# A hybrid decoder step on Trainium2: where 13 fill steps and one tile's weights lie in the mLSTM recurrence

## The chip, the cores and the metric

The kernel runs on one core of one Trainium2 chip. The metric is the device time of one execution, in microseconds (us). A core has several engines that run side by side, each with its own stream of instructions: TensorE (PE) multiplies matrices into PSUM banks and loads the weights for that (PEld), VectorE (DVE) and ScalarE (ACT) do elementwise work and empty PSUM, GpSimd (POOL) does elementwise work too and issues transfers, SyncE (SP) only issues transfers (DMAs). They wait for one another on semaphores.

## The reference

One inference step of a two-layer decoder: an mLSTM layer, then a forgetting-attention layer over one shared K/V, each followed by a SwiGLU FFN. A prompt of 1024 tokens (with 16 meta tokens ahead of it) and 8 requests of 8 new tokens go through the same weights. The change lies in the mLSTM layer, whose mixer is:

```python
def mlstm_chunk(state, inp):
    C, n, m = state
    ...
    s = jnp.einsum('bhtk,bhsk->bhts', q, k) * jnp.exp(dmat - m_t[..., None])
    num = w_inter[..., None] * jnp.einsum('bhtk,bhkv->bhtv', q, C) + jnp.einsum('bhts,bhsv->bhtv', s, v)
    den = w_inter * jnp.einsum('bhtk,bhk->bht', q, n) + jnp.sum(s, axis=-1)
    h = num / jnp.maximum(jnp.abs(den), jnp.exp(-m_t))[..., None]
    ...
    C_new = w_c[..., None, None] * C + jnp.einsum('bhs,bhsk,bhsv->bhkv', w_g, k, v)
    ...
def mlstm_mixer(xn, C0, n0, m0, lead, w_in, b_ig, b_fg, mh_g, w_out):
    p = xn @ w_in
    ...
    h, state = mlstm_sequence(q, k, v, li, lf, state0, lead)
    h = rmsnorm(h.transpose(0, 2, 1, 3), mh_g)
    out = (h.reshape(B, T, HV).astype(xn.dtype) * jax.nn.sigmoid(og)) @ w_out
    return out, state
```

`D_MODEL` is 1024, with 8 mLSTM heads of key width 64 and value width 128. The output gate `og` is a 1024 x 1024 part of the projection `xn @ w_in`. It doesn't depend on the recurrence, only its use does.

## The kernel before

The 1104 tokens (64 of the samples, 16 meta, 1024 of the prompt) lie in nine chunks: chunk 0 has the samples and the meta tokens, 80 in all, and chunks 1 to 8 have 128 each. For the large products they are taken in three groups of three chunks, t = 0, 1, 2, of 336, 384 and 384 columns. To keep float32 accuracy each operand is split into a high and a low part, and each product is three matmuls (`mm3`, lines 193 to 195, the high part of the weights twice, and the low part).

The mixer first makes values, then queries and keys, which go to memory (`qkD`). Then comes `recurrence`, chunk by chunk. For each chunk `chunk_load` brings queries and keys (`qk`), the rows of decays (`eb`) and the weights of the queries (`wb`); `chunk_decay` and an exp make the decay matrix; `chunk_scores` multiplies keys with queries into `sps`, multiplies that with the decay on DVE (L1351), transposes the keys into `kps` (L1355), and scales keys (`kw`, L1357) and queries (`wb`, L1359); `chunk_state` makes the products `cp` for the next state C, and lets POOL decay it (L1395); `chunk_out` makes the products `nps` (from the chunk, and from the state), which ACT copies over the values `vA` (L1420) before it takes the sums of squares (`jk`). Chunk 0 also has the samples, each with its own state `C0`. For them `first_queries` writes the scaled queries to memory (`qwD`, L1367) and reads them back in another layout (`qq`, L1371), and in `chunk_out` DVE places them (L1433) before PE multiplies them with `C0` (L1438).

These products are small and wait for one another. Between them stands **fill**: the output gate's projection, written as a generator, `gates_out`. It has 8 weight tiles, m = 0 to 7, by 3 token groups, by 8 steps, 192 steps in all. One step is three matmuls. Eight steps make one PSUM tile `mmA`; then ACT takes the sigmoid into a staging tile `stg`, and POOL issues its write to memory (`ogD`, L956). The staging tiles are a ring of three. `mmA` has two PSUM banks. `f(n)`, or `g(n)`, called somewhere in the code, issues n steps there. The weights of tile m + 1 are loaded while tile m is in its second group: SP loads them, ACT makes the high part, DVE the low part (L272).

In the last two chunks another piece of work joins. `gate(t)` takes one head of a finished group of chunks, transposes its three chunks into one bank (`ghps`, L1555, which takes its turn in the same two banks as the fill's `mmA`), multiplies it with the gate that was read back from memory (L1556, into `ogqk` or `ogeb`), and splits the product (L271, L272) into the operands of the next stage. In these chunks `g` is defined anew: it calls `gate` each time it is called, and in chunk 8 two fill steps ahead of that. Just before, at the end of chunk 6, a loop issues fill until only the last tile's last group is left (the 184 of the loop's bound).

Within the recurrence the order on PE, DVE, ACT and POOL is that of the code (a manual schedule). Waits come from the data and from memory that is taken over: a tile that lies where an earlier one lay waits for the last use of that one.

The next stage (`mlp`, its products are `pops`) multiplies the gated heads with `w_out`. Its eight weight pairs, m = 0 to 7, high and low, were prepared earlier and are loaded by SP, in order (L512):

```python
for m in range(KT):
    for z in range(2):
        nc.sync.dma_start(ws[m][z].bitcast(F32), self.woD[m][:, z])
```

Pairs 0 to 3 are the tiles `wo2` on the left side of memory, pairs 4 to 7 lie in the `slots` on the right side. The left ones take the memory where the weights of the recurrence's fill and its staging ring had been: pairs 0 and 1 lie over weights, pair 2 over the staging ring. The stage also brings the residual `hD` into the memory of the values (L499, on POOL).

The change touches `gates_out` (its weights' place), `recurrence` (how many steps stand where), `chunk_scores`, `first_queries`, `chunk_state` and `chunk_out`.

Of the kernel before, what the change touches and what calls it, by code (L numbers as in the profile page):

```python
# [12 lines left out]
ALU = mybir.AluOpType  # L13
# [4 lines left out]
P = 128  # L18
D = 1024
KT = D // P  # L20
# [8 lines left out]
NT = len(TT)  # L29
# [8 lines left out]
HA, DK, DV = 8, 64, 128  # L38
# [841 lines left out]
def phase_a(self, vt):  # L880
    nc, I, O = self.nc, self.I, self.O
    w_in = I["w_in_a"][0]
# [3 lines left out]
    with ExitStack() as c3:  # L886
# [48 lines left out]

        def gates_out():

            get = lambda m, later=None: self.load_w([w_in[:, (16 + m) * P : (17 + m) * P]], later=later)
            ws = [get(0)]
            later = []  # L940
# [211 lines left out]
def recurrence(self, kp, rec, v, qkD, fill, gate):  # L1152


    nc, I, O = self.nc, self.I, self.O
    eD, wD, cap, cap0, wcP, wcS, bm = rec
# [4 lines left out]
    def f(n):  # L1161
        for _ in range(n):
            next(fill, None)
            self.fills += 1
# [3 lines left out]
    with ExitStack() as cr, self.pool("recAp", bufs=2, space=PSUM) as pp:  # L1168
# [28 lines left out]
        with self.pool("rec2") as sets[2], self.pool("rec1", bufs=2) as rp, self.pool("rec3") as sets[0]:  # L1197
# [8 lines left out]
            for i in range(1, NT):  # L1206
                N2 = load(i + 2) if i + 2 < NT else None
                if i + 1 < NT:
                    f(12 if i == 1 else 3)
                    self.chunk_scores(i + 1, N, rp, *args, f)  # L1210
# [21 lines left out]
                if i == 6:  # L1232
                    while self.fills < 3 * KT * KT - KT:
                        f(1)

                    def g(n):
                        if i == NT - 1:
                            f(2)
                        gate(0) or gate(1)
                R, N = N, N2  # L1240
# [98 lines left out]
def chunk_scores(self, i, R, rp, pp, kp, C, v, qkD, eD, wD, tm, f):  # L1339
# [10 lines left out]
    for g in range(2):  # L1350
        nc.vector.tensor_tensor(out=eb[:L, g::2, :L], in0=sps[g][:L, :, :L], in1=eb[:L, g::2, :L], op=ALU.mult)  # L1351
    f(2 if i else 6)
# [6 lines left out]
    nc.vector.tensor_tensor(out=qw[:, :, :L], in0=qk[:, :4, :L], in1=qw[:, :, :L], op=ALU.mult)  # L1359


@_add(Net)
def first_queries(self, R, sp):

    nc = self.nc
    qd = self.dram.tile([P, 4, NS], F32, name="qwD")
    nc.gpsimd.dma_start(qd, R["qw"][:, :, :NS])  # L1367
    q2 = R["q2"]
    for a in range(2):
        for z in range(2):  # L1370
            nc.gpsimd.dma_start(q2[a * 64 : a * 64 + 64, :, z, :], qd[z * 64 : z * 64 + 64])  # L1371
    for qm in R["qms"]:
        nc.gpsimd.memset(qm, 0.0)


@_add(Net)
def chunk_state(self, i, R, pp, kp, C, v, qkD, eD, wD, tm, wcP, f):
# [15 lines left out]
    if i + 1 < NT:  # L1393

        nc.gpsimd.tensor_tensor(out=Cw, in0=Cn, in1=wcP[:, :, i].unsqueeze(2).broadcast_to([P, 4, DV + 1]),  # L1395
                                op=ALU.mult)
# [3 lines left out]
def chunk_out(self, i, R, rp, pp, kp, C, v, qkD, eD, wD, tm, den, ssq, f, sp=None, exp=None, then=None):  # L1400
# [22 lines left out]
    if i == 0:  # L1423
        for g, hs in enumerate(((0, 2), (4, 6), (1, 3), (5, 7))):
            f(4)
# [13 lines left out]
            done(ps, g, hs)  # L1439
    else:  # L1440

        for z in range(2):
            f(2 if z == 0 else 3)
# [1596 lines left out]
```

## Time and profile before

| | us |
|---|---|
| median of 3 runs (lowest, highest) | 2829.18 (2827.18, 2837.07) |
| the profiled execution | 2829.72 |
| its span | 2828.0 |
| PE busy, share of the span | 2761.9 (98%) |
| DVE busy | 1800.4 (64%) |
| ACT busy | 1177.3 (42%) |
| POOL busy | 836.0 (30%) |
| mean granted TensorE clock | 0.994 |

The span is the time between the first and the last instruction of the profiled execution; 1.72 us of its time lie outside. Busy time is summed for each engine and says nothing about what it worked beside. Rows of groups give line, engine, operation and tiles (out<-in), the count, the busy time, the mean of one, and what ended the idle time before them, with its amount in brackets. In the timeline the first number is the time in the span, the second the busy time of the piece. `PEclk` is the TensorE clock that was granted, as a share of full speed. Where several instructions run into each other, as PE's matmuls do, a duration contains overlap with its neighbours, and the distance between starts is the pitch.

### The profile page before, as it was taken

What the parts mean: (1) busy time and instruction counts of PE and PEld (TensorE: products, weight loads), DVE (VectorE), ACT (ScalarE), POOL (GpSimd) and SP (SyncE); (2) the same over time, 40 slices, a digit from 0 to 9 for tenths busy, and PEclk for the clock granted to TensorE, in tenths of its full rate; (3) what the DMA queues carried; (4) which work ended last, traced back from release to release, by engine and by line L of the source; (5) the groups of instructions that cost most, each with busy time, mean ns of one, the idle gap of its engine ahead of it and who ended that gap; (6) DMA issues with size and microseconds to landing.
All of it is one profiled execution on the core that took longest, in us unless ns stands there. A gap on an engine that the chain in (4) does not pass through costs nothing. (4 is left out here: it accounts for less than half of the span.)

```text
span 2828.0 us, 60538 instructions
## 1 busy us (share of the span) xinstructions
PE 2761.9 (98%) x23543; PEld 2650.3 (94%) x23543; DVE 1800.4 (64%) x4025; ACT 1177.3 (42%) x2299; POOL 836.0 (30%) x1313
## 2 busy tenths in 40 slices
PE   8999999999999999999999999999999999999998
PEld 8989889999999999999999888677999999999998
DVE  4632566888887765563455444777388888766556
ACT  5422453432322334443444445777343223323345
POOL 3122233132232332124453202544313223323111
PEclk9999999999999999999999999999999999999999
DMA  6666547245554375545444676442524555527556
GB/s 196 171 196 162 144 125 255 90 143 165 176 167 148 112 243 174 195 145 171 139 172 132 237 279 226 154 143 86 157 83 128 175 176 164 161 90 239 178 191 215
DMA packets 439001, 474.03 MB, mean 168 GB/s; under 512 B 41422, under 2 KB 365258, under 8 KB 437690
## 3 DMA queue, kind: packets, MB, share of 16 engines
q1 hardware_dynamic: 387522, 320.78, 36.8%
q0 software_dynamic: 43808, 143.17, 15.3%
q10 hardware_dynamic: 7384, 6.22, 0.7%
q8 instruction: 185, 3.03, 0.5%
q14 instruction: 102, 0.84, 0.1%
HBM read 322.84 MB, written 147.21 MB: 166 GB/s over the span
## 5 line engine op out<-in xcount | busy, mean ns | idle before, releaser
L1611 PE MATMUL m<-xh,slot 128*128 128x276 f32 x2752 | 541.3, 290 | 1.8 <-ACT fs L1640 1.8
L1611 PEld LDWEIGHTS m<-xh,slot 128*128 128x128 f32 x2752 | 440.4, 188 | 3.6 <-ACT fs L1640 2.2
L1611 PE MATMUL m<-xl,slot 128*128 128x276 f32 x1376 | 397.4, 289 | 0.0
L1611 PEld LDWEIGHTS m<-xl,slot 128*128 128x128 f32 x1376 | 259.1, 188 | 0.0
L193 PE MATMUL tmps<-slot,xh 128*128 128x256 f32 (+2 forms) x864 | 243.1, 281 | 0.0
L195 PE MATMUL tmps<-slot,xl 128*128 128x256 f32 (+2 forms) x864 | 240.6, 278 | 0.0
L194 PE MATMUL tmps<-slot,xh 128*128 128x256 f32 (+2 forms) x864 | 240.5, 278 | 0.0
L272 DVE TENSOR_TENSOR slot<-slot,slot 128x1024 fp32r<-128x1024 f32 x124 | 162.9, 1314 | 60.7 <-ACT slot L271 59.2
L271 ACT CAST slot<-slot 128x1024 fp32r<-128x1024 f32 x124 | 129.6, 1046 | 141.2 <-PE m L1611 111.7
L194 PEld LDWEIGHTS tmps<-slot,xh 128*128 128x128 f32 (+1 forms) x864 | 159.2, 184 | 0.1
L195 PEld LDWEIGHTS tmps<-slot,xl 128*128 128x128 f32 (+1 forms) x864 | 158.6, 184 | 0.0
L193 PEld LDWEIGHTS tmps<-slot,xh 128*128 128x128 f32 (+1 forms) x864 | 158.4, 183 | 0.2
L193 PE MATMUL mmA<-xh,whi 128*128 128x384 f32 (+1 forms) x384 | 135.1, 352 | 0.0
L194 PE MATMUL mmA<-xl,whi 128*128 128x384 f32 (+1 forms) x384 | 127.9, 333 | 0.0
L195 PE MATMUL mmA<-xh,wlo 128*128 128x384 f32 (+1 forms) x384 | 127.7, 333 | 0.0
L272 DVE TENSOR_TENSOR slot<-vA,slot 128x1024 fp32r<-128x1024 f32 (+1 forms) x59 | 82.2, 1396 | 32.6 <-ACT slot L271 31.5
L272 DVE TENSOR_TENSOR slot<-Ht,slot 128x1024 fp32r<-128x1024 f32 (+1 forms) x59 | 81.4, 1382 | 32.3 <-ACT slot L271 31.1
L271 ACT CAST slot<-Ht 128x1024 fp32r<-128x1024 f32 (+1 forms) x59 | 61.0, 1037 | 96.8 <-PE m L1611 92.9
L271 ACT CAST slot<-vA 128x1024 fp32r<-128x1024 f32 (+1 forms) x59 | 60.8, 1035 | 95.5 <-PE m L1611 90.5
L1715 DVE TENSOR_TENSOR ws<-ws 128x128 f32<-128x128 f32 x264 | 93.8, 355 | 8.9
L2862 ACT ACTIVATE s<-s,nb 128x272 f32<-128x272 f32 (+7 forms) x126 | 98.9, 786 | 0.0
L2897 ACT COPY th<-tp 128x768 f32<-128x768 f32 (+1 forms) x80 | 73.6, 920 | 53.7 <-PE tp L2889 30.5
(805 smaller groups left out, 8668.8 us busy)
## 6 DMA issues: line engine op xcount, KB each, us to landing
ws<-in_w_down SPq DMA_DIRECT2D x176, 128.0 KB, 2.8
sD<-ws SPq DMA_DIRECT2D x176, 128.0 KB, 2.3
slot<-sD SPq DMA_DIRECT2D x40, 512.0 KB, 4.2
slot<-in_w_gate_up SPq DMA_DIRECT2D x36, 512.0 KB, 3.9
kp<-in_cache_k SPq DMA_DIRECT2D x32, 512.0 KB, 6.7
vp<-in_cache_v SPq DMA_DIRECT2D x32, 512.0 KB, 5.1
vA<-in_w_gate_up SPq DMA_DIRECT2D x26, 512.0 KB, 4.4
Ht<-in_w_gate_up SPq DMA_DIRECT2D x26, 512.0 KB, 3.9
```

What stands on the lines that cost most here:

```text
L193: mm(ps, sh, mh, start=first, stop=False)
L194: mm(ps, sh, ml, start=False, stop=False)
L195: mm(ps, sl, mh, start=False, stop=last)
L271: self.nc.scalar.copy(hi, src)
L272: self.nc.vector.tensor_tensor(out=lo, in0=src, in1=hi.bitcast(F32), op=ALU.subtract)
L1611: nc.tensor.matmul(u.ps[h, b], w[p][:, k], x[q][:, k], start=first and k == i == 0, stop=k == 3 and i == 2, skip_group_check=True)
L1715: tt(out=o, in0=a, in1=b, op=ALU.subtract)
L2862: nc.scalar.activation(ss[z, u], ss[z, u], AF.Exp, bias=nb[:, z : z + 1], accum_out=sm[:, u, z : z + 1])
L2897: nc.scalar.copy(th.rearrange("p x z (u h q) -> p h (x z u) q", h=2, q=64)[:, :, :n], pt[:, :, :n])
```

## The change

- **Weights of m = 7.** A new pool, `gl`, on the right side of memory, takes the high and the low tile of m = 7. They lie where two of the later `slots` are, the low parts of weight pairs 6 and 7 of the next stage.
- **Fill.** Chunk 1 issues 10 steps instead of 12 ahead of chunk 2's scores, chunks 2, 4 and 5 issue 2 instead of 3 there. In `chunk_out` the first half has 1 step instead of 2 in chunks 1, 2, 4 and 5, and in chunk 0 the first of each group's calls has 3 instead of 4. The loop that issued fill at the end of chunk 6 is gone. In the last two chunks, `g` issues one step (chunk 7) or two (chunk 8) before each gate. By the end of chunk 6, 186 steps had been issued before, and 173 now.
- **First queries.** In chunk 0 the queries are scaled ahead of the six fill steps instead of behind the keys; in `first_queries` the two memsets stand ahead of the four reads, which now go by half (z) first; and the first decay of the state on POOL moves from `chunk_state` to `chunk_out`, behind the second of four groups.

```diff
+        gl = c3.enter_context(self.pool("gl", side="right"))
...
-            get = lambda m, later=None: self.load_w([w_in[:, (16 + m) * P : (17 + m) * P]], later=later)
+            get = lambda m, later=None: self.load_w([w_in[:, (16 + m) * P : (17 + m) * P]], later=later,
+                                                    keep=gl if m == 7 else None)
...
-                    f(12 if i == 1 else 3)
+                    f(10 if i == 1 else 2 if i in (2, 4, 5) else 3)
...
                 if i == 6:
-                    while self.fills < 3 * KT * KT - KT:
-                        f(1)
 
                     def g(n):
-                        if i == NT - 1:
-                            f(2)
+                        f(2 if i == NT - 1 else 1)
                         gate(0) or gate(1)
...
+    scale = lambda: nc.vector.tensor_tensor(out=qw[:, :, :L], in0=qk[:, :4, :L], in1=qw[:, :, :L], op=ALU.mult)
+    if i == 0:
+        scale()
     f(2 if i else 6)
...
-    nc.vector.tensor_tensor(out=qw[:, :, :L], in0=qk[:, :4, :L], in1=qw[:, :, :L], op=ALU.mult)
+    if i:
+        scale()
...
-    for a in range(2):
-        for z in range(2):
-            nc.gpsimd.dma_start(q2[a * 64 : a * 64 + 64, :, z, :], qd[z * 64 : z * 64 + 64])
     for qm in R["qms"]:
         nc.gpsimd.memset(qm, 0.0)
+    for z in range(2):
+        for a in range(2):
+            nc.gpsimd.dma_start(q2[a * 64 : a * 64 + 64, :, z, :], qd[z * 64 : z * 64 + 64])
...
-        nc.gpsimd.tensor_tensor(out=Cw, in0=Cn, in1=wcP[:, :, i].unsqueeze(2).broadcast_to([P, 4, DV + 1]),
-                                op=ALU.mult)
+        decay = lambda: nc.gpsimd.tensor_tensor(out=Cw, in0=Cn, in1=wcP[:, :, i].unsqueeze(2).broadcast_to(
+            [P, 4, DV + 1]), op=ALU.mult)
+        if i:
+            decay()
+        else:
+            R["decay"] = decay
...
-            f(4)
+            f(3)
...
             done(ps, g, hs)
+            if g == 1:
+                R["decay"]()
...
-            f(2 if z == 0 else 3)
+            f(3 if z else 1 if i in (1, 2, 4, 5) else 2)
```

The order that results, at three places. First POOL in chunk 0, around the write of the first queries; `qk`, `eb` and `wb` in the last rows are the loads for chunk 1. Before:

```order
L956 DMA ogD<-stg_3194 128x384
L1367 DMA qwD<-wb_3080 512x1x64
L1371 DMA qq<-qwD 64x4x64 x4
L1373 MEMSET qq 128x400 x2
L1395 TENSOR_TENSOR C_107<-C_105,wcP 128x516
L1279 DMA qk_3246<-qkD 128x8x128
L1278 DMA eb_3086<-eD 128x8x128
L1283 DMA wb_3247<-wD 64x4x128 x2
```

And now:

```order
L959 DMA ogD<-stg_3198 128x384
L1371 DMA qwD<-wb_3083 512x1x64
L1374 MEMSET qq 128x400 x2
L1377 DMA qq<-qwD 64x4x64 x4
L1279 DMA qk_3248<-qkD 128x8x128
L1278 DMA eb_3089<-eD 128x8x128
L1283 DMA wb_3249<-wD 64x4x128 x2
L959 DMA ogD<-stg_3264 128x384
L1398 TENSOR_TENSOR C_107<-C_105,wcP 128x516
```

The write of the queries keeps its place behind a write of the gate, the memsets stand ahead of the reads, and the decay of the state (`C_107`) has moved behind the loads of chunk 1 and one more write of the gate.

Second, PE in chunk 7 and 8, from the fifth gate's transposes to chunk 8's state products (`mmA_260` and `mmA_267` are the last tile's groups t = 1 and t = 2 of the changed kernel; the last group of the kernel before is `mmA_262`). Before:

```order
L1555 MATMUL ghps_267_4818<-ident_60,vA_96 128x80
L1555 MATMUL ghps_267_4818<-ident_60,vA_96 128x128 x2
L193 MATMUL mmA_262_4666<-xh_91,whi_253_4353 128x384
L194 MATMUL mmA_262_4666<-xl_92,whi_253_4353 128x384
L195 MATMUL mmA_262_4666<-xh_91,wlo_254_4354 128x384
L1555 MATMUL ghps_269_4852<-ident_60,vA_96 128x80
L1555 MATMUL ghps_269_4852<-ident_60,vA_96 128x128 x2
L1388 MATMUL cp80_4859<-vA_96,kw8_4547 64x129 x4
L1388 MATMUL cp81_4865<-vA_96,kw8_4547 64x129 x4
```

And now:

```order
L1564 MATMUL ghps_265_4793<-ident_60,vA_96 128x80
L1564 MATMUL ghps_265_4793<-ident_60,vA_96 128x128 x2
L193 MATMUL mmA_260_4692<-xh_91,whi_253_4449 128x384
L194 MATMUL mmA_260_4692<-xl_92,whi_253_4449 128x384
L195 MATMUL mmA_260_4692<-xh_91,wlo_254_4450 128x384
L193 MATMUL mmA_267_4827<-xh_91,whi_253_4449 128x384
L194 MATMUL mmA_267_4827<-xl_92,whi_253_4449 128x384
L195 MATMUL mmA_267_4827<-xh_91,wlo_254_4450 128x384
L1564 MATMUL ghps_268_4831<-ident_60,vA_96 128x80
L1564 MATMUL ghps_268_4831<-ident_60,vA_96 128x128 x2
L1392 MATMUL cp80_4838<-vA_96,kw8_4502 64x129 x4
L1392 MATMUL cp81_4844<-vA_96,kw8_4502 64x129 x4
```

The last step of group t = 1 and the first of t = 2 stand where one step of t = 2 stood, and the sixth gate's transposes (`ghps_268`, before `ghps_269`) follow on a tile of group t = 1 that is only just complete.

ACT at the start of chunk 7, from chunk 6's last squares (`jk66`, `jk67`) to the split of the first gate (`ogqk6`) and chunk 7's copies. Now (the kernel before has the same rows in the same order, without the two of L958):

```order
L1478 ACTIVATE jk66_4656,ssqA_104<-vA_96 128x128
L1478 ACTIVATE jk67_4658,ssqA_104<-vA_96 128x128
L958 ACT_TABLE_LOAD
L958 ACTIVATE stg_259_4677<-mmA_258_4613 128x336
L271 CAST xh_91<-ogqk6_4662 128x336 x2
L1427 COPY vA_96<-nps70_4739 128x2x128
L1427 COPY vA_96<-nps71_4740 128x2x128
```

The sigmoid of the last tile's group t = 0, with a load of ACT's function table, has moved behind the squares.

Third, POOL at the end of the recurrence; `vA<-hD` is the residual's load for the next stage, the rows to `out_p_C` and `out_p_n` write the last state. Before:

```order
L971 DMA ogqk7_4841<-ogD_98 128x384 x2
L956 DMA ogD_98<-stg_268_4849 128x384
L499 DMA vA_96<-hD_87 128x8x276
L1253 DMA out_p_C<-C0_105 64x4x128 x2
L1261 DMA out_p_n<-noP_4933 4x128
```

And now:

```order
L974 DMA ogqk7_4816<-ogD_98 128x384 x2
L959 DMA ogD_98<-stg_266_4824 128x384
L1253 DMA out_p_C<-C0_105 64x4x128 x2
L499 DMA vA_96<-hD_87 128x8x276
L959 DMA ogD_98<-stg_272_4924 128x384
L1261 DMA out_p_n<-noP_4936 4x128
```

The write of the last staging tile stood ahead of the residual's load, and stands behind it now.

## The prediction

> **What bounds the kernel now.** I read the page's totals first, then TensorE (PE) in the stretch that the diff touches, in windows of 3.4 us.
>
> ```profile
> span 2828.0 us, 60538 instructions
> ...
> PE 2761.9 (98%) x23543; PEld 2650.3 (94%) x23543; DVE 1800.4 (64%) x4025; ACT 1177.3 (42%) x2299; POOL 836.0 (30%) x1313
> ```
>
> PE is the bound: it idles 66 us in all, so a change of order can win only PE's waits near the recurrence, or add some. The profiled execution took 2829.72 us, 0.54 above the median of the runs (2829.18). The windows show the two places where PE starves, and the price:
>
> ```profile
> core 0: us, PE busy (x) PEld busy (x) DVE busy (x) ACT busy (x) POOL busy (x), PEclk, DMA share, GB/s
> ...
> 254.26:257.67 3.41, 1.57 (x11) 1.28 (x9) 0.98 (x1) 0.49 (x1) 3.41 (x6) 1.00 0.28 79
> 257.67:261.08 3.41, 2.92 (x13) 2.95 (x14) 1.13 (x4) 0.00 (x0) 3.41 (x6) 0.50 0.48 131
> 418.10:421.50 3.40, 2.25 (x27) 1.89 (x23) 1.74 (x10) 2.96 (x8) 0.48 (x2) 1.00 0.89 257
> 421.50:424.93 3.43, 1.53 (x14) 0.93 (x11) 2.63 (x9) 1.21 (x4) 2.33 (x4) 1.00 1.03 418
> 424.93:428.34 3.41, 3.41 (x21) 2.88 (x19) 1.82 (x5) 1.29 (x4) 0.00 (x0) 0.50 1.02 389
> ```
>
> Twice a window in which PE was busy less than half (1.57 and 1.53 us) is followed by one at clock 0.50; after 2.25 us it is not. A halved window full of work loses half of 3.41, 1.7 us. So a wait costs itself, and 1.7 more if it leaves one window under about half.
>
> **Part A, first queries sooner.** Chunk 0's products with the sample state need the copy of the queries.
>
> ```profile
> 249.33 0.54 POOL L956 DMA_DIRECT2D ogD<-stg  x1 [3.31 <-ACT stg L955]
> 250.84 0.74 POOL L1367 DMA_DIRECT2D qwD<-wb  x1 [0.97 <-DVE wb L1359]
> ...
> 253.51 2.48 POOL L1371 DMA_DIRECT2D qq<-qwD  x4 [1.92 <-DMA qwD<-wb]
> ...
> 256.75 1.06 POOL L1395 TENSOR_TENSOR C<-C,wcP 128x516 f32<-128x516 f32 x1
> ...
> 256.69 2.21 DVE L1433 COPY qq<-qq 64x32 f32<-64x32 f32 x4 [5.56 <-DMA qq<-qwD]
> ...
> 262.42 0.80 DVE L1433 COPY qq<-qq 64x32 f32<-64x32 f32 x4
> ...
> 255.52 0.32 PE L195 MATMUL mmA<-xh,wlo 128*128 128x336 f32 x1
> ...
> 258.16 1.98 PE L1438 MATMUL nps<-C,qq 128*80 128x129 f32 x8 [2.33 <-POOL C L1395]
> ```
>
> PE waited 2.33 us. The query product moves ahead of f(6) on DVE, but on POOL qwD still stands behind the gate write of 249.33, which ends at 249.87: the write can start 0.7 to 0.97 us sooner, not more. Both z=0 transfers are then issued first, and the first four copies no longer share their time with the decay: 2.21 us there against 0.80 alone, half of it before the first product. That is up to 0.7 more. Bounds: 0 (another transfer lands last) and 1.7; I take 1.3, near the upper since both delays stand in rows. The wait becomes 2.33 - 1.3 + 0.53 (one step fewer ahead of it) = 1.6 us, right at the half-window limit, so its halved window stays or goes: 0 to 1.7 gained, I take half, 0.85. The memsets now lie under qwD's flight (1.92 us of idle POOL against two of 0.4), and cost nothing. The decay behind gate 2 has until chunk 1's state, tens of us; the chunk-1 loads behind it come sooner. A = -2.15 (0 to -3.4).
>
> **Part B, 13 steps leave chunks 0 to 6.** One step is three matmuls of 384 columns, of which 18 in a row give the pitch:
>
> ```profile
> 397.45 0.44 PE L193 MATMUL mmA<-xh,whi 128*128 128x384 f32 x1
> ...
> 400.51 0.34 PE L195 MATMUL mmA<-xh,wlo 128*128 128x384 f32 x1
> ...
> 376.77 1.29 DVE L1351 TENSOR_TENSOR eb<-sps,eb 128x512 f32<-128x512 f32 x2 [3.22 <-ACT eb L1335]
> ...
> 377.77 0.60 PE L1355 MATMUL kps<-ident,qk 128*128 128x128 f32 x4
> ```
>
> (400.51 - 397.45)/17 = 0.18, so 0.53 a step. Twelve (the thirteenth is in A) give -6.4 there, if their cover wasn't needed. In chunk 5, DVE's first half of L1351 ends at about 377.45 (half of 1.29, with the overlap) and kps takes its bank at 377.77: a margin of 0.3 us, from which f(2) in place of f(3) takes 0.53. So 0.2 lost at i = 2, 4 and 5 each; the z=0 steps have other work behind them. I take +0.6 (0 to 1.5, the upper if each removed step there turned into wait). B = -5.8.
>
> **Part C, chunks 7 and 8, where they come back.** Times here are on the clock of before; A and B move them all by the same amount.
>
> ```profile
> 407.40 0.60 PE L1355 MATMUL kps<-ident,qk 128*128 128x128 f32 x4
> 407.84 0.46 PE L1555 MATMUL ghps<-ident,vA 80*128 80x80 f32 x3
> ...
> 417.02 0.48 PE L1555 MATMUL ghps<-ident,vA 80*128 80x80 f32 x3 [0.26 <-DVE ogqk L1556]
> ...
> 419.68 0.51 PE L1555 MATMUL ghps<-ident,vA 80*128 80x80 f32 x3 [1.15 <-DVE ogqk L1556]
> ...
> 423.10 0.55 PE L1555 MATMUL ghps<-ident,vA 128*128 128x128 f32 x3 [0.93 <-DVE ogeb L1556]
> 424.62 1.84 PE L1450 MATMUL nps<-vA,eb 128*128 128x129 f32 x8 [0.97 <-ACT vA L1420]
> ...
> 428.31 0.38 PE L193 MATMUL pops<-xh,wo 128*128 128x276 f32 x1
> ...
> 408.32 0.19 ACT L1469 ACTIVATION_READ_ACCUMULATOR jk<-vA 128x1 f32 x1
> ...
> 419.01 1.28 ACT L955 ACT_TABLE_LOAD   x1
> 420.30 0.49 ACT L955 ACTIVATE stg<-mmA 128x384 f32<-128x384 f32 x1
> ```
>
> The gate heads' transposes (ghps) and the fill share two PSUM banks (mmA). In chunk 7 the first ghps now needs the bank of the fill tile that ends ahead of chunk 8's scores, and ACT evacuates it only behind chunk 6's eight squares (end 408.51), with a table load of 1.28 and a sigmoid of 0.45: 410.26. PE arrives one step after kps, at about 408.5: **a new wait of 1.8 us**. At the sixth ghps the same happens: its bank holds m=7's t=1 tile, whose sigmoid stands behind five gates and four squares on ACT. From the first ghps to the end of that sigmoid it was 420.79 - 407.84 = 12.95; the table load falls away (the set is in), 11.67, so 422.0 on the new start. PE's own work there is 9.5 (five ghps of 0.4, cp 1.0, two nps pairs of 1.63, six steps of 0.53, 0.3 of small waits): **1.9 us of wait**. Behind it the fill hides all old waits: 417.02 to 428.31 is 11.29, less 1.15, 0.93 and 0.97 of waits and 1.5 of halved clock, 6.7; with seven steps 10.4. Pops starts at 422.0 + 10.4 = 432.4 against 428.31, +4.1 (bounds +2.3 without the first wait, +6.4 if no idle time takes a step). Each of the two waits leaves a window under half if it falls inside one, which is about even: +1.8 (0 to 3.4). C = +5.9.
>
> By the Trainium skill, TensorE: Matmul & The Clock Gate, section Why this matters for your kernels, PE should avoid idle gaps over about 3 us between bursts; shorter ones would then be free of the clock. The halved window after a wait of 2.33 us above disagrees; by the rule C would be 1.8 less.
>
> **Part D, the weights of the next stage.** The next stage (pops) reads eight weight pairs, m=0 to 7, loaded by SP in order.
>
> ```profile
> 416.84 11.62 SPq L512 DMA_DIRECT2D wo<-woD  x8
> ...
> wo<-woD SPq DMA_DIRECT2D x4, 512.0 KB, 9.4
> ...
> wraw<-in_w_in_a SPq DMA_DIRECT2D x9, 512.0 KB, 4.6
> vA<-hD POOLq DMA_DIRECT2D x4, 1104.0 KB, 6.9
> ...
> ogD<-stg POOLq DMA_DIRECT2D x16, 192.0 KB, 2.3
> ...
> 426.38 1.23 PE L1454 MATMUL nps<-C,wb 64*128 64x129 f32 x8
> ...
> 427.84 0.65 ACT L1420 COPY vA<-nps 128x256 f32<-128x256 f32 x2 [1.02 <-DVE den L1412]
> ...
> 434.76 0.38 PE L193 MATMUL pops<-xh,wo 128*128 128x276 f32 x1
> ```
>
> With m=7's weights on the right, pairs 0 and 1 no longer wait for the last fill (416.84 before) but for m=6's, some 15 us sooner. Pair 2's memory lies over the staging tiles of the gate (stg), so it waits until the *last* stg has been written out, and that is now at the end of chunk 8. With Q the end of chunk 8's nps (427.61 on the old clock): ACT copies to Q + 0.9, sigmoid to Q + 1.4, write issued Q + 1.7, landed 2.3 later if nothing is ahead of it; but vA<-hD (1104 KB, 6.9 us) was issued on the same queue some 3 us before Q, so Q + 4.2. Then 4.6 for the first half of pair 2 and 1.35 for the second (512 KB at 389 GB/s): Q + 10.2, with SP's issue of 0.1. PE needs it after a step, a ghps, a small transpose and two units (434.76 - 428.31 = 6.45): Q + 7.8. Before, the same load was issued 1.4 us ahead of Q. **A wait of 2.4, up to 3.6 where the first load takes a us more;** I take 3.0, since those four loads took 9.4 in a full queue and 4.6 is an empty one's. Its lower bound is 0 (write and load both faster). It leaves a window under half: +1.7 (0 to 1.7). Pairs 3 to 7 come at 2.7 us a pair against 3.4 of PE, so nothing waits behind. D = +4.7.
>
> **Sum.** -2.15 - 5.8 + 5.9 + 4.7 = +2.65, the profiled execution 2832.4, the median 0.5 lower: 2832. All engines stand in the same order from the pops on, so nothing is added later.
>
> **Rivals.**
> - *Net gain.* A in full (-3.4), B without loss (-6.4), C without halved clock (+4.1), D's wait 1.5 without its clock: -4.2, median 2825. For it: each term is at its row's bound, none beyond; it decides if the write of the last stg lands within 3 us of Q. Against it: vA<-hD ahead of that write.
> - *Even.* The skill's rule holds for short waits: C is +4.1, the sum +0.85, the median 2830. Against it stands the window at 257.67.
> - *Clearly slower.* The remaining loads come slower than PE reads them: if a 512 KB load takes 2.4 us instead of 1.35 under the gate loads (ogc), a pair takes 4.8 against 3.4, 1.4 lost at each of five pairs, +7 on top: +9.7, 2839. It decides from 1.7 us a load. For it: DMA is at 1.02 here; against: a halved backlog, with pairs 0 and 1 gone.
> - *No sooner query.* A = 0: +4.8, 2834; if qwD's write, behind the gate write on POOL, starts no earlier.
>
> **Chances.** Forecast (2830 to 2836, with the query rival in it) 0.57; gain 0.25; even 0.08; clearly slower 0.10. 0.5% is 14 us, about what a measurement of this kernel can tell from no change (the three runs span 10 us); no gain reaches it, and of the slower case three in ten could. Faster 0.01, same 0.95, slower 0.04. The range goes from the gain's 2825 to the slow loads' 2839, which leaves out about 0.15.
>
> **What would show it.** A: L1438 first starts 1.3 us sooner relative to the qwD write's predecessor, with 1 to 2 us of wait. B: chunks 1 to 6 some 6 us shorter. C: two waits near 2 us on ghps, put down to ACT's stg, no waits for ogqk or ogeb, one table load less in chunk 8. D: a pops wait of about 3 us at m=2, ended by a DMA. I am wrong if ghps doesn't wait for stg, if pops runs through, or if waits appear behind the pops.

## The result and the profile after

The changed kernel takes 2836.41 us against 2829.24 before (medians of 12 runs each). The ratio is 1.0023, with a 95% interval of 1.0014 to 1.0031: 6.5 us slower, 4.0 to 8.8, or 0.2%. One of the changed kernel's runs was slow, 3875.49 us at a mean granted clock of 0.643; the ratio and its interval leave it out (the median of the other eleven is 2836.08). The result lies within the forecast range (2825 to 2839) and on the forecast side, but 4.4 us above the forecast time of 2832, and just above the band of 2830 to 2836 in which the prediction saw its own case. The profiled execution took 2838.73. Of the 9.0 us between the two profiled executions 2.0 lie ahead of the recurrence, in a stretch that the change doesn't touch: chunk 0's scores (the first `sps`) start at 244.34 us in the kernel before and at 246.35 now. So everything below is measured from there.

The view of windows, for the kernel before, cut at the starts on PE of chunk 0's scores, chunk 1's scores, chunk 8's scores, the next stage (first `pops`) and that stage's fifth unit. A unit is the 24 products with one weight pair; the last stretch holds four of them, m = 0 to 3 (the texts of expectations call this stretch the first three units). The first column is the window, the second its length, then the busy time of each engine, the granted clock, the DMA share and GB/s:

```profile
244.34:308.34 64.00, 61.67 (x391) 54.18 (x390) 28.04 (x86) 19.51 (x40) 16.98 (x28) 0.97 0.45 119
308.34:405.16 96.82, 96.31 (x759) 87.50 (x759) 57.09 (x136) 52.96 (x145) 35.57 (x49) 1.00 0.46 132
405.16:428.32 23.16, 17.96 (x158) 14.67 (x157) 15.12 (x44) 12.92 (x44) 7.00 (x11) 0.93 0.58 201
428.32:441.55 13.23, 13.23 (x108) 13.23 (x106) 10.75 (x29) 6.02 (x17) 4.29 (x7) 1.00 1.02 393
```

The same four stretches of the changed kernel:

```profile
246.35:306.16 59.81, 58.45 (x379) 50.96 (x379) 29.23 (x86) 19.33 (x40) 17.05 (x28) 1.00 0.48 129
306.16:400.47 94.31, 92.12 (x733) 82.67 (x732) 57.00 (x136) 53.23 (x143) 32.97 (x45) 1.00 0.50 143
400.47:431.08 30.61, 26.40 (x197) 22.45 (x196) 16.36 (x46) 13.87 (x46) 8.80 (x15) 0.89 0.39 119
431.08:450.49 19.41, 16.20 (x109) 15.65 (x106) 10.62 (x28) 6.47 (x18) 5.37 (x9) 0.82 0.89 331
```

Chunk 0 is 4.2 us shorter and chunks 1 to 7 are 2.5 shorter. Chunks 7 and 8, behind the last scores, are 7.45 longer and the first four units of the next stage 6.2. The sum is 204.14 against 197.21, +6.9, and behind it the two executions run alike (2386.4 and 2386.5 us to the end). In the two longer stretches the granted clock falls to 0.89 and 0.82. What PE waits for from 200 to 480 us, from the view of waits of the changed kernel (total, times, longest, in us); the rows of `ghps` and `pops` are the waits of these two stretches:

```profile
PE ghps L1564 <- ACT stg L958: 3.9, 2, 2.2
PE pops L193 <- DMA wo<-woD: 2.0, 1, 2.0
PE nps L1445 <- issue: 1.3, 1, 1.3
PE pops L195 <- DMA wo<-woD: 1.2, 1, 1.2
PE kps L1358 <- DVE eb L1351: 1.1, 2, 0.9
PE nps L1459 <- ACT vA L1427: 1.0, 2, 0.7
```

The old waits for `ogqk` and `ogeb` (5.2 us with the `nps` wait among them) are gone but for 0.3 us. In their place are two waits for a staging tile and two for the next stage's weights. The sigmoids that end the first two, the issues of the residual's load and of the last staging tile's write, and the first products behind each wait:

```profile
404.10 1.28 ACT L958 ACT_TABLE_LOAD   x1
405.39 0.45 ACT L958 ACTIVATE stg<-mmA 128x336 f32<-128x336 f32 x1
...
418.95 0.47 ACT L958 ACTIVATE stg<-mmA 128x384 f32<-128x384 f32 x1
...
427.45 0.90 POOL L499 DMA_DIRECT2D vA<-hD  x1 [2.96 <-PE ghps L1564]
432.00 0.57 POOL L959 DMA_DIRECT2D ogD<-stg  x1 [3.65 <-ACT stg L958]
...
405.99 0.79 PE L1564 MATMUL ghps<-ident,vA 80*128 80x80 f32 x3 [2.15 <-ACT stg L958]
...
419.56 0.77 PE L1564 MATMUL ghps<-ident,vA 80*128 80x80 f32 x3 [1.78 <-ACT stg L958]
...
439.79 0.39 PE L193 MATMUL pops<-xh,wo 128*128 128x276 f32 x1 [2.03 <-DMA wo<-woD]
...
441.57 0.60 PE L195 MATMUL pops<-xh,wo 128*128 128x276 f32 x1 [1.19 <-DMA wo<-woD]
```

The windows around them, on the grid on which the clock changes:

```profile
402.54:405.95 3.41, 1.29 (x9) 0.93 (x8) 1.80 (x3) 3.27 (x13) 0.00 (x0) 1.00 0.48 175
405.95:409.36 3.41, 3.37 (x21) 2.74 (x22) 1.81 (x4) 0.47 (x1) 0.58 (x2) 0.50 0.15 55
416.19:419.60 3.41, 1.49 (x9) 0.88 (x8) 2.19 (x10) 2.70 (x12) 1.48 (x3) 1.00 0.61 187
419.60:423.01 3.41, 3.41 (x22) 2.75 (x23) 1.98 (x5) 0.47 (x1) 0.55 (x1) 0.50 0.17 62
436.67:440.08 3.41, 1.38 (x11) 1.14 (x10) 3.41 (x5) 0.00 (x0) 0.00 (x0) 1.00 1.00 337
440.08:443.49 3.41, 2.23 (x10) 1.92 (x10) 1.57 (x4) 1.27 (x3) 1.32 (x2) 0.50 1.03 419
443.49:446.91 3.42, 3.42 (x17) 3.42 (x16) 0.00 (x0) 0.00 (x0) 0.00 (x0) 0.50 1.02 396
```

Each of the three long waits leaves PE busy for 1.29 to 1.49 us of a window, and each is followed by a window at half clock. The third is followed by two.

### The profile page after: what moved, and what is told of

Its sections match the earlier page's. It is cut to its first block, busy times and chain, and to the rows that moved or that the text cites. A ratio compares the mean times of both kernels' runs of the same rounds, so it can differ in the third digit from the quotient of the medians.

```text
span 2837.0 us, 60539 instructions
## 1 busy us (share of the span) xinstructions
PE 2767.9 (98%) x23543; PEld 2654.5 (94%) x23543; DVE 1800.3 (63%) x4025; ACT 1178.3 (42%) x2300; POOL 833.8 (29%) x1313
## 5 line engine op out<-in xcount | busy, mean ns | idle before, releaser
L1724 DVE TENSOR_TENSOR ws<-ws 128x128 f32<-128x128 f32 x264 | 93.7, 355 | 8.8
```

What stands on the lines that cost most here:

```text
L1724: tt(out=o, in0=a, in1=b, op=ALU.subtract)
```

## The experiments

Each table row gives the four stretches of one kernel as in the windows above, their sum, the median of its runs and its ratio to the kernel before, measured beside it. The stretches are from one profiled execution each and tell parts of a microsecond; the medians have an interval of some 3 us to each side. Each row has a kernel before of its own, so two rows are compared by their ratios; where the two intervals overlap widely, only the stretches tell a difference. The sum leaves out what stands behind the fourth unit, 2384.6 to 2392.7 us in these traces. Windows at half clock come and go there, and the rest of that spread was not followed up.

| kernel | chunk 0 | chunks 1-7 | chunks 7, 8 | four units | sum | median | ratio (95%) |
|---|---|---|---|---|---|---|---|
| before | 64.0 | 96.8 | 23.2 | 13.2 | 197.2 | 2829.2 | |
| changed | 59.8 | 94.3 | 30.6 | 19.4 | 204.1 | 2836.4 | 1.0023 (1.0014-1.0031) |
| e1 queries alone | 61.4 | 96.8 | 22.5 | 13.9 | 194.5 | 2826.7 | 0.9987 (0.9977-0.9997) |
| e2 fill back | 61.3 | 101.2 | 23.2 | 13.2 | 198.9 | 2833.1 | 1.0012 (1.0003-1.0021) |
| e3 weights left | 59.7 | 95.3 | 35.2 | 17.0 | 207.2 | 2838.4 | 1.0033 (1.0021-1.0045) |
| e4 staging tile right | 60.1 | 95.3 | 30.6 | 13.2 | 199.3 | 2831.4 | 1.0005 (0.9996-1.0014) |
| e5 three steps back | 60.0 | 95.3 | 24.6 | 20.6 | 200.4 | 2834.1 | 1.0024 (1.0012-1.0035) |
| e6 = e4 + e5 | 60.2 | 96.7 | 24.2 | 13.2 | 194.4 | 2827.5 | 0.9988 (0.9979-0.9998) |
| e7 dummies | 60.1 | 94.3 | 29.1 | 17.8 | 201.3 | 2832.8 | 1.0014 (1.0005-1.0023) |
| e8 = e6 + pair order | 59.9 | 97.0 | 24.5 | 14.0 | 195.5 | 2827.9 | 0.9992 (0.9983-1.0002) |
| e9 = e6 + one step moved | 59.8 | 94.6 | 24.5 | 13.2 | 192.1 | 2825.0 | 0.9990 (0.9980-1.0001) |
| e10 = e2 + pair order | 61.3 | 96.8 | 25.4 | 19.2 | 202.7 | 2835.4 | 1.0020 (1.0010-1.0031) |
| e11 = e9 + two steps moved | 59.7 | 93.7 | 24.6 | 13.2 | 191.2 | 2823.5 | 0.9973 (0.9962-0.9984) |

The account to be tested was the prediction's: each wait stands where it says, and a wait costs itself and a window of halved clock if it empties one by more than half. Its rivals were that the clock doesn't hang on these waits, and that a wait once removed comes back elsewhere.

### e1: the first queries alone

The kernel before with the new order in `chunk_scores`, `first_queries` and `chunk_state`, and nothing else (to the changed kernel):

```diff
-        gl = c3.enter_context(self.pool("gl", side="right"))
...
-                                                    keep=gl if m == 7 else None)
+                                                    keep=None)
...
-                    f(10 if i == 1 else 2 if i in (2, 4, 5) else 3)
+                    f(12 if i == 1 else 3)
...
-                        f(2 if i == NT - 1 else 1)
+                        if i == NT - 1:
+                            f(2)
...
-            f(3)
+            f(4)
...
-            f(3 if z else 1 if i in (1, 2, 4, 5) else 2)
+            f(3 if z else 2)
```

The loop at the end of chunk 6 is not put back: 186 steps are issued by then, its bound of 184 is passed, and it would issue none.

> The first queries' part alone (scaling ahead of the fill, memsets ahead of the reads, reads by half, decay of the state later); the fill steps and the weights' place as before. My account: the first product with the sample states waits 1.0 us where it waited 2.33, the halved clock behind it goes, so from chunk 0's scores to chunk 1's it is 61.0 us against 64.0 before and 59.8 in the changed kernel, all else as before: 2826. Rival, that the queries come no sooner and only the fill step taken away shortened that stretch: 64.0, and 2829.

Chunk 0 took 61.4 us and the whole 2826.69: this part alone is a gain of 3.7 us (0.8 to 6.5). In the timeline of e1, PE's first product with a sample state now waits 1.09 us instead of 2.33, and no halved clock follows:

```profile
254.14 1.08 PE L1445 MATMUL nps<-C,qq 128*80 128x129 f32 x8 [1.09 <-issue]
```

In the changed kernel the same can be followed through the engines. First the write that stands ahead of the queries' on POOL, then DVE's copies and PE's product:

```profile
251.34 0.54 POOL L959 DMA_DIRECT2D ogD<-stg  x1 [3.32 <-ACT stg L958]
...
257.48 0.17 DVE L1440 COPY qq<-qq 64x32 f32<-64x32 f32 x1 [3.19 <-DMA qq<-qwD]
258.06 0.94 DVE L1440 COPY qq<-qq 64x32 f32<-64x32 f32 x3 [0.41 <-DMA qq<-qwD]
...
258.69 1.08 PE L1445 MATMUL nps<-C,qq 128*80 128x129 f32 x8 [1.32 <-issue]
```

From the gate's write to the product it is 7.35 us, against 8.83 before (258.16 - 249.33): 1.5 sooner. Of this 1.2 stand ahead of DVE's first copy (6.14 against 7.36). The four copies take 1.1 us where they took 2.2 beside POOL's decay. The parts of the new order (the scaling, the memsets and reads, the decay) were not run apart, and the view put the old wait down to the decay on POOL. That the queries themselves came sooner is read from the copies.

### e2 and e10: the weights' new place, with the fill put back

e2 is the changed kernel with all fill steps where they were (the last four pieces of the diff above). e10 gives, besides, the tile over the staging ring to weight pair 0:

```diff
-                ws = [ws[x] for x in (3, 2, 1, 0)] + held if heads else held + ws
+                ws = [ws[x] for x in (1, 3, 2, 0)] + held if heads else held + ws
```

> The changed kernel with all fill steps where they stood before (the first queries' part and the new place of the last tile's weights stay). My account: the weights' place only lets the first two weight pairs of the next stage load sooner, which nothing waited for; 61.0 us in chunk 0, 23.2 from chunk 8's scores to the next stage, 13.2 for its first three units, and 2826, as for the queries' part alone. Rival, that the tiles on the right make the late weight pairs wait, whose memory they take: waits at the seventh or eighth unit, 2830 or more.

> All fill steps as before, the queries' part, the last tile's weights on the right (as in the run with the fill put back, 2833), and the tile over the staging ring given to weight pair 0, so that no pair loads before the last staging tile is written, in chunk 8. If the pairs' transfers in chunk 6 held up chunk 8's decays there (11.1 us from issue to landing, against 6.7 without them): DVE's wait of 3.7 us and PE's of 3.2 with its halved clock go, from chunk 1's scores to chunk 8's 96.8 us against 101.2, and 2826 to 2828, the time of the queries' part alone. If the tiles' place on the right costs by itself: 2831 or more.

Both accounts of e2 were wrong. Chunk 0 and the next stage came out as expected, but chunks 1 to 7 took 4.4 us more than in e1, at a place that neither account had named. From the views of e2 (PE's waits, DVE's timeline, and the DMA issues in the stretch from 386.5 to 388):

```profile
PE nps L1460 <- ACT vA L1428: 3.1, 1, 3.1
...
398.43 2.19 DVE L1333 SCALAR_TENSOR_TENSOR eb<-eb,tmA,cap 128x128 f32<-128x128 f32 x8 [3.71 <-DMA eb<-eD]
...
eb<-eD POOLq DMA_DIRECT2D x1, 512.0 KB, 11.1
```

With the last tile's weights out of the way, the first two weight pairs of the next stage (four loads of 512 KB on SP's queue) are released in chunk 6, 2.6 us ahead of the load of chunk 8's decays. That load lands 11.1 us after its issue, against 6.6 in e10 below. DVE, in order, waits for it with the copies of chunk 6's denominators behind it, ACT waits for those, and PE for ACT: 3.1 us, and a halved window. In e10 no pair loads in chunk 6:

```profile
eb<-eD POOLq DMA_DIRECT2D x1, 512.0 KB, 6.6
```

DVE's wait is gone and chunks 1 to 7 take 96.8 us, as the account said. The total was a miss all the same: the pairs, all behind the last staging tile now, were issued 7.1 us ahead of the next stage's first product, against 11.5 in the kernel before, and its first unit waited 3.6 + 2.6 us. In the changed kernel the pairs load at 394, when the decays have landed. There DVE doesn't wait for them, and the collision plays no part in the loss.

### e3: the last tile's weights on the left

```diff
-                                                    keep=gl if m == 7 else None)
+                                                    keep=None)
```

> The changed kernel with the last tile's weights on the left as before, so that the first two weight pairs of the next stage wait for the last fill matmul, at the end of chunk 8. My account: 5.0 us for the first half of pair 0 and 1.3 for the second, behind a wait that ends with chunk 8: 5 to 6 us of PE's wait at the first unit instead of 3.2 at the third, with one or two halved windows: 20 to 22 us for the first three units against 19.4, and 2838. The wait of DVE for chunk 8's decays (eb) in chunk 6, if there is any in the changed kernel, goes, since the pairs no longer load there. Rival, that the pairs' place doesn't count because the staging ring holds them anyhow: 19.4, 2836.

2838.4, as expected: PE waits 4.2 + 1.7 us at the first unit, where it waited 2.0 + 1.2 at the third. The 4.2 stand ahead of the first `pops` and count with chunks 7 and 8 in the table. So with steps at the end of chunk 8 the new place of the weights is worth 3.1 us by the stretches; the medians lie 2.0 apart, and the ratios (1.0033 and 1.0023, with intervals that overlap) barely tell the two kernels apart. With the fill where it was it costs, as e2 shows against e1.

### e4: the last staging tile elsewhere

```diff
-                            s = st.tile([P, GL], F32, name=self.uid("stg"), tag="stg")
+                            s = (gl if m == 7 and t == 2 else st).tile([P, GL], F32, name=self.uid("stg"), tag="stg",
+                                                                       bufs=1 if m == 7 and t == 2 else None)
```

> The changed kernel with the last group's staging tile in the pool on the right, so that the third weight pair's memory is free once the group before it has been written out. My account: the wait at the third unit (3.2 us in all) and the halved clock behind it go, the first three units take 13.2 us against 19.4, the rest stays: 2830. Rival, that the pair would be late anyhow (its load stands behind the residual's and the gates' loads): 17 to 19 us for these units, 2835.

The third unit's wait and its halved clock are gone: 13.2 us for the four units, and 2831.4. The staging tile under pair 2 was the cause.

### e5 and e6: the group t = 0 complete by the end of chunk 6

```diff
-                    f(10 if i == 1 else 2 if i in (2, 4, 5) else 3)
+                    f(10 if i == 1 else 3)
```

> The changed kernel with three steps instead of two ahead of the scores of chunks 3, 5 and 6, so that 176 steps are issued by the end of chunk 6 and the group t = 0 of the last tile is complete, its sigmoid ahead of the squares on ACT. My account: the waits of 2.2 and 1.8 us for a staging tile go with their halved clocks, a new one of about 1.6 comes in chunk 7 where the sigmoid of t = 1 stands behind two copies and a table load; the keys' transposes no longer wait; from chunk 8's scores to the next stage 24 to 26 us against 30.6; the last sigmoid stands some 4 us sooner, and the third unit's wait goes too: 2823 to 2826. Rival, that the waits only move to the next staging tile: 29 us or more in the last two chunks, 2835.

> The 176 steps by the end of chunk 6 (the run with three steps ahead of the scores of chunks 3, 5 and 6) together with the last staging tile on the right. There the third unit waited 5.0 us, since the write of the last staging tile (issued 0.9 us behind the residual's load) landed 6.0 us after its issue, against 2.4 in the changed kernel. My account: this wait and its halved clock go, the first three units take 13.2 us against 20.6; the wait of 1.7 us in chunk 6 stays; 2825 to 2827. Rival, that the next weight pairs are as late: 17 us or more, 2830.

In e5 chunks 7 and 8 took 24.6 us (24 to 26 expected), but the whole 2834.1, where 2823 to 2826 were expected; by the ratios (1.0024 and 1.0023) it is as slow as the changed kernel. The two waits for a staging tile have become one of 0.8 us, no window there is halved, and `kps` waits for nothing. But the third unit's wait, which was to vanish, grew to 4.0 + 0.9 us. The last staging tile's write was issued earlier, but nearer behind the residual's load (DMA issues of e5 in the stretch 419 to 421.5):

```profile
vA<-hD POOLq DMA_DIRECT2D x1, 1104.0 KB, 6.4
ogD<-stg POOLq DMA_DIRECT2D x1, 192.0 KB, 6.0
```

And of the changed kernel, from 431 to 433, where the residual had been issued 4.5 us ahead:

```profile
ogD<-stg POOLq DMA_DIRECT2D x1, 192.0 KB, 2.4
```

In e5 the write lands 0.5 us behind the residual, as it does in e6 (8.9 and 8.5 us from issue to landing): it waits for the larger transfer of its own queue. In e6, which joins e4 and e5, this no longer matters: 13.2 us for the four units, 2827.5. This is 8.9 us less than the changed kernel.

### e7: more work on PE, in the wait

```diff
+                        if heads and (t, m) == (0, 2):
+                            for k in range(2 * KT):
+                                nc.tensor.matmul(ps[:, :SL], ws[1][0][:, k % KT], self.X[0][0][:, k % KT], start=True, stop=True)
                         self.fm_cols(ps[:, :SL], *ws[m], self.X[t])
```

> The changed kernel with 16 more matmuls of 276 columns (2.2 us, their result overwritten) on PE ahead of the third unit of the next stage, in the wait of 2.0 + 1.2 us for its weights. If the halved clock of 6.8 us behind that wait comes from PE's idle window, it goes: the second wait of 1.2 stays, the first three units take 16.4 us against 19.4, and 2833.4, with more work on PE. If the clock has another cause (the transfers, or the time since the last idle stretch): 19.4 to 19.6, and 2836.5.

With 16 useless matmuls in the wait the kernel takes 2832.8 (2833.4 expected). The four units take 17.8 us, 1.6 less than without the matmuls. The medians lie 3.6 apart, but the ratios (1.0014 and 1.0023) don't tell the two kernels apart. Its windows around the two places:

```profile
398.78:402.19 3.41, 2.40 (x17) 1.92 (x14) 2.58 (x4) 3.39 (x18) 0.29 (x1) 1.00 0.78 285
402.19:405.60 3.41, 2.28 (x25) 1.92 (x26) 1.22 (x3) 1.45 (x3) 0.55 (x1) 1.00 0.16 55
405.60:409.01 3.41, 3.34 (x28) 2.74 (x26) 2.24 (x7) 1.12 (x3) 2.11 (x3) 1.00 0.15 33
...
432.91:436.32 3.41, 2.72 (x22) 2.50 (x21) 3.41 (x6) 0.27 (x1) 0.00 (x0) 1.00 0.95 319
436.32:439.73 3.41, 2.04 (x14) 1.81 (x14) 1.17 (x2) 1.00 (x3) 1.32 (x2) 1.00 1.03 397
439.73:443.14 3.41, 3.41 (x30) 3.41 (x29) 1.23 (x3) 0.95 (x2) 0.75 (x1) 1.00 1.00 383
```

The last three rows are the next stage: PE is busy for 2.04 us or more of each window, and the clock stays at 1.00, with the DMA share as high as before. So the halved clock there comes from PE's idle time and not from the transfers. 16.4 us were expected for the four units; the weights landed 0.8 us later behind the start of the stage, and PE waited 2.1 us beside the useless matmuls. That the total came out as expected is luck: 1.4 us more here, and 1.5 less in chunks 7 and 8, for another reason. The first three rows are a second, unplanned answer. The first wait for a staging tile is as long as in the changed kernel (2.1 us), but the grid line at 402.19 cuts it in two. Both windows keep over 2.2 us of work, and no halving follows; these chunks took 29.1 us against 30.6.

### e8 and e9: chunk 8's decays

e5 and e6 have a wait of 1.7 and 1.6 us (0.3 in the changed kernel) at chunk 6's products with the values, behind a late load of chunk 8's decays. e8 takes the weight pairs out of chunk 6 (e6 with the order of tiles of e10), e9 moves one step from chunk 5 to chunk 6:

```diff
-                    f(10 if i == 1 else 3)
+                    f(10 if i == 1 else 2 if i == 5 else 4 if i == 6 else 3)
```

> As the run before it, and the tile over the staging ring is given to weight pair 0 instead of pair 2, so that all eight pairs wait for the staging tile of t = 1, in chunk 7. Where the first two pairs load in chunk 6, DVE waited for chunk 8's decays (3.7 us with the fill as before and the weights on the right, 1.9 with 176 steps), and PE behind it for the values (3.2 and 1.7 us). My account: both come from the pairs' 2 MB on the DMA engines ahead of the decays; they go, and nothing new waits: 1.7 us less than the run before it, 2823 to 2825. Rival, that the decays are late for another reason: the wait stays; or that the loads now delay the gates read back in chunk 7: new waits of 1 to 3 us there, 2826 or more.

> 176 steps by the end of chunk 6 and the last staging tile on the right, as in the run that joined the two, but one step moved from chunk 5 to chunk 6 (two ahead of chunk 6's scores, four ahead of chunk 7's). With 160 steps, a whole number of tiles, by the end of chunk 5 there, a gate's write stood on POOL just ahead of the loads for chunk 8 and waited for its sigmoid; the decays' load was issued 1.0 us behind the start of chunk 7's scores, against 2.3 ahead of it in the changed kernel, and DVE waited 1.8 to 2.1 us for it, PE 1.6 to 1.9 behind DVE, whether or not the weight pairs loaded there. With 159 the write comes behind the loads. My account: DVE's wait for the decays and PE's wait go, with the halved clock behind it where there was one; from chunk 1's scores to chunk 8's 93.5 us against 96.7, and 2823 to 2825. Rival, that another load or the sigmoid in its new place (behind chunk 5's squares, with a table load) makes DVE or PE wait as long: 95.5 or more, 2826 to 2828.

In e8 no pair loads in chunk 6, and the wait stays (DVE 2.1 us, PE 1.9): here the pairs were not the cause, and the account taken over from e2 fell. The later pairs brought new waits, 0.6 us at the third unit and 1.3 at a gate behind the fourth. POOL's timeline in e8 shows another:

```profile
381.94 0.61 POOL L960 DMA_DIRECT2D ogD<-stg  x1 [6.03 <-ACT stg L959]
...
383.55 0.90 POOL L1279 DMA_DIRECT2D eb<-eD  x1
```

POOL waits for the sigmoid of a fill tile that is complete with the last step of chunk 5, and the loads for chunk 8 stand behind that write. The decays are issued 1.0 us behind the start of chunk 7's scores (382.58). In e9 that write comes later, and the decays are issued 2.9 us ahead of those scores (386.02), when their memory comes free:

```profile
383.09 0.88 POOL L1279 DMA_DIRECT2D eb<-eD  x1 [3.73 <-PE nps L1460]
```

DVE doesn't wait for them, no window is halved, and chunks 1 to 7 take 94.6 us instead of 96.7. 93.5 were expected: `kps` waits 0.2 us in chunk 5, where the step was taken away, and `nps` 0.7 in chunk 3 and 0.5 in chunk 6. The median is 2825.0. The ratios of e6 and e9 don't tell the two apart (0.9988 and 0.9990); the 2.1 us are shown by the stretches alone.

### e11: two more steps into chunk 0's wait

```diff
-                    f(10 if i == 1 else 2 if i == 5 else 4 if i == 6 else 3)
+                    f(8 if i == 1 else 2 if i == 5 else 4 if i == 6 else 3)
...
-            f(3)
+            f(3 if g else 5)
```

> The run with the step moved to chunk 6, and two more steps moved: five instead of three ahead of chunk 0's first group, where PE waits 1.3 us for the queries, and 8 instead of 10 ahead of chunk 2's scores, where it doesn't wait. If a wait is worth what can be put in it: chunk 0 stays near 59.8 us with a wait of 0.3, from chunk 1's scores to chunk 2's it is 6.7 against 7.8, and 1 us less than that run, 2824. Rival, that the steps ahead of chunk 2's scores cover something (the keys or the decay of chunk 2): a wait of 0.5 or more there, and 2825, no change.

From chunk 1's scores to chunk 2's it is 6.8 us, chunk 0 stays at 59.7, and its wait is 0.4. The whole, 2823.5, is 0.27% below the kernel before, with an interval of 0.16 to 0.38%. It beats both kernels. The profiled execution, 2828.69, is the slowest of its seven; behind the four stretches it is 4.7 us longer than the kernel before, and why was not followed up. Its four stretches:

```profile
244.71:304.44 59.73, 59.33 (x386) 51.77 (x385) 28.16 (x86) 19.61 (x41) 17.23 (x28) 1.00 0.49 129
304.44:398.11 93.67, 92.28 (x737) 83.33 (x736) 56.47 (x136) 53.22 (x143) 32.73 (x45) 1.00 0.53 151
398.11:422.66 24.55, 21.86 (x188) 18.46 (x187) 14.81 (x42) 13.45 (x44) 9.59 (x16) 1.00 0.57 189
422.66:435.87 13.21, 13.21 (x109) 13.21 (x106) 10.90 (x31) 6.44 (x18) 4.25 (x7) 1.00 0.88 272
```

The clock is 1.00 in all four. Of the 6.0 us between 197.2 and 191.2, 3.5 are PE's idle time (length less busy, 4.5 us here and 8.0 before), and 2.5 its busy time, which no window at half clock stretches here.

## Why the prediction was right, and where its sizes were off

The direction and the places were right: two waits for a staging tile, one for the third weight pair, the old waits hidden, the queries sooner. e1, e4 and e5 bear out the queries, the staging tile under the third pair and the place of the sigmoids, each by itself. The prediction's sum was +2.65 us, the stretches give +6.9, and the difference lies in two kinds of terms.

- **Part A** was put at -2.15 and is -2.65 by e1 (64.0 to 61.35), a little better than the sum had it. In the changed kernel chunk 0 is 4.2 shorter, of which 1.6 are three of part B's steps. The product came 1.5 us sooner, for 1.3 forecast. The halved window goes in every profiled execution with this part, where the prediction took half of it.
- **Part B** was put at -6.4 + 0.6, and is -4.1: 1.6 in chunk 0, and 2.5 in chunks 1 to 7, where nine steps should give 4.8. The cover that the steps had given was sized too small: 0.6 was taken, and idle time there rose by 1.7 (0.5 to 2.2, length less busy), most of it before `kps` (1.1) and `nps`. The row chosen for the margin, 0.3 us in chunk 5, didn't stand for the other places: in chunk 5 `kps` waits for nothing, in chunk 2 for 0.23 us and in chunk 4 for 0.85, where 0.2 were taken for each. In e5, e6 and e11, with three or two of the steps back ahead of the scores, the waits for `kps` are 0.2 at most.
- **Part C** was put at +4.1 and +1.8 for the clock, and is +7.45. The waits are 2.15 and 1.78 us, for 1.8 and 1.9 forecast. The term that was off is the clock: the prediction said that it is about even whether such a wait leaves a window under half, and took one window of two; here both were halved (+3.4). e7 shows that it does hang on the grid, since there the first of the two was not. Two small slips of the working change little: its terms for PE's own work add up to 9.7 us and not 9.5 (1.9 of wait goes with 9.7), and half of 3.4 is 1.7.
- **Part D** was put at 3.0 + 1.7 and is 6.2: a wait of 3.2, but two halved windows instead of one. In the first of them PE was busy for 2.23 us, at half clock, and the second followed. The residual's load, which the prediction had in front of the write, was not in the way in the changed kernel (2.4 us from issue to landing). That the write landed 4.3 us behind chunk 8's products, with 4.2 forecast, is in part luck, since the forecast had it wait for the residual. That the residual can be in the way is shown by e5 (6.0).

So the terms that were mis-sized are the price of the halved clock, taken at half a window for each of C's waits and at one for D's, where four windows came and about two were summed (some 3 us over C and D), and B's cover (1.7). Less the 0.5 of A they make the 4.3 us between the sum and the stretches. As for the rivals: e7 and the windows of the changed kernel speak against the even case, in which short waits don't touch the clock. The gain needed the last write landed within 3 us of chunk 8's products, and it took 4.3. The case without a sooner query fell with e1. The rule of the Trainium skill (TensorE: Matmul & The Clock Gate, section Why this matters for your kernels), by which gaps over about 3 us are the ones to avoid, isn't borne out as a limit by these runs: waits of 1.8 and 2.15 us were each followed by 3.41 us at 0.50. The remaining loads came no slower than PE read them, as the forecast said: behind the third unit no unit waits, which speaks against the clearly slower case. In e4, e6 and e9 a later unit or two wait 0.5 to 0.8 us in all.

Open is why `nps` waits for the values in chunk 3, between 0.65 and 1.8 us in the kernels with moved steps, with as many steps in that chunk as before (0.25). In e3 and e4, which have the 1.8, DVE waited 0.7 us for a load of decays shortly before; where it is 0.7, as in the changed kernel, DVE did not wait there.

## What to carry to other kernels

Ahead of a bound engine, filler is worth moving only into waits, and its products' way counts as much as its place: the eviction, the write, the memory that the write frees, and whatever stands behind them in a queue. Look which step completes a tile; one step more or less put a sigmoid ahead of eight squares, or a write behind a load. And price a short wait on PE at up to one or two windows of halved clock, by how much of a window it leaves empty, before it is called hidden.

## What the runs showed that was not expected

- The clock goes by windows of 3.41 us on a fixed grid. In all thirteen traces, with the windows worked out along the grid from 200 to 2750 us, every window at full clock in which PE was busy for at most 1.58 us was followed by one at half clock. From 1.62 to 1.79 us it went both ways, and from 1.82 on none was, but for one of 2.53 us (e8) and three of 2.94 (e3, e5, e6), which are not explained. So in these traces the limit lies near half of a window. In a window that is itself at half clock the busy time alone doesn't tell what follows: 2.77 us (e3, e11) and 2.92 (the kernel before, at 257.67) were enough for full clock, and 2.23 (the changed kernel), 2.80 (e10) and 3.00 (e8) were not. What counts there was not tested.
- A wait of the same length cost 1.5 us less when the grid line fell inside it (e7 against the changed kernel, chunks 7 and 8).
- A transfer of 192 KB landed 2.4 us after its issue, and 6.0 where 1104 KB had been issued on its queue 0.9 us ahead. A load of 512 KB from POOL's queue landed after 6.6 us, and after 11.1 with four loads of 512 KB issued on SP's queue just ahead: another queue was no protection. e10 against e2 shows it, since only the pairs' order differs.
